# The first stage of a transformer layer reordered: inputs loaded in another order, one tile's modulation moved from TensorE to VectorE, and two blocks normalized from a transposed copy

## The chip, the cores and the metric

The kernel runs on one core of a Trainium2 chip. The metric is the time of one execution in microseconds (us) of device time; for the kernel before it is the median of three runs. Engines are called as the profile does: PE is TensorE's matmul, PEld its weight load, DVE VectorE, ACT ScalarE, POOL GpSimd, SP the engine that issues the DMAs. A transpose is a matmul against the identity matrix and so runs on PE.

## The reference

One layer of a transformer trunk, one sequence of S = 2048 tokens, D = 1024 features, everything in float32. Cut to what is computed:

```python
mod_all = einsum('bd,lde->lbe', silu(c), ada_w) + ada_b        # six rows of 1024
sh_m, sc_m, gt_m, sh_f, sc_f, gt_f = split(mod_all)
h = rms_norm(x, g0) * (1 + sc_m) + sh_m                        # norm over the 1024 features
y = stick_breaking_attention(h)                                # 16 heads of 64, w_qkv, w_o
x = x + gt_m * rms_norm(y, g1)
h = rms_norm(x, g2) * (1 + sc_f) + sh_f
x = x + gt_f * rms_norm(swiglu(h), g3)                         # w_in, w_out
```

The change lies in the first three lines and in what follows them at once, the products of h with the query, key and value weights. The modulation is 1 + scale times the gain (`g_eff`, one number for each feature) and the shift (`mod`).

## The kernel before

**Layout and precision.** The 2048 tokens are four blocks b = 0 to 3 of 512; the 1024 features are eight tiles k (or m) = 0 to 7 of 128. The products want h with the features on the 128 partitions, so a tile of h is 128 features x 512 tokens. Every float32 product is made of three matmuls on halves: each operand is split into a high part (a cast, on ACT) and a low part (a subtraction, on DVE or POOL), and `mm3` (L174 to L176) adds high x high, high x low and low x high. Three such rows are called a triple below. The heads go by pairs p = 0 to 7; t = 1, 0, 2 are the projections to k, q and v, in that order.

**The start, block 0** (L776 to L930). `row_load(m)` fetches the columns of ada_w for feature tile m, shift and scale, 512 KB each (ar). For the first `COLUMNS` tiles (three) the sums over c are made on PE as 16 matmuls of 128x1 a tile (`column`, L708, acol); for the other tiles DVE multiplies the rows with silu(c), spread over all partitions (c_rows), and adds up (`row_sum`, L716). silu(c) is made by ACT's Silu function; the spreading is done by two matmuls with ones (cs, L806). `row_done` makes mod and g_eff of the tile. Block 0's x comes by tokens (x0_0 to x0_3): `x_square` makes the squares' sum on ACT and the reciprocal root on POOL, `x_scale` multiplies on DVE, `turn_x(m)` transposes a tile by four transposes on PE, `full(m)` applies g_eff and mod on ACT, `high(m)` casts and `low(m)` subtracts. `products(p, m)` then issues the triples of tile m for the head pairs p = 0 and 1.

**Block 1 and block 3, by features** (`BY_FEATURES`). The host lays out a second copy of x with the features first (xt); its tiles (xc) need no transposes. Only the row of reciprocal roots has to come from x by tokens: the square sums of four token tiles (L165), each spread to 128 columns (`x_spread`, L340), four transposes to one row on all partitions (xr, `x_share`, L352) and a copy by ACT (L354). Then `scale_cols` multiplies xc by g_eff and the row (L372 on DVE, L376 on POOL) and `modulate` adds the shift with the cast (L389, L394, L395) and subtracts (L390, L397).

**Block 2, by tokens.** Its four token tiles are squared on ACT (xj, L165), scaled in place on DVE (L338), and transposed by 32 transposes on PE (xT2, L361), four ahead of each use; ACT applies g_eff and mod (L383), DVE casts and subtracts (L384, L385).

**What sets the order.** The instructions of PE, ACT, DVE and POOL run in the order in which the program writes them, each engine in order by itself; an engine that waits holds all that stands behind it on that engine. The start is straight-line code. From there on a loop goes through steps (p, b), each with t = 1, 0, 2 and k = 0 to 7 (`project`); block 1's step with p = 0 follows the start, then blocks 2 and 3; `first_norm(b, k)` makes the tiles of the next block beside the products of the present one. From block 1's t = 2 on, attention work of earlier blocks is put between the triples: scores z, the scan w (DVE), the product a (POOL), transposes t and their halves aT (ACT and DVE), the outputs o. SP issues the DMAs in program order, and each buffer's load waits until its earlier reader is done.

Of the kernel before, what the change touches and what calls it, by code (L numbers as in the profile page):

```python
# [16 lines left out]
P = 128  # L17
D = 1024
# [21 lines left out]
COLUMNS = 3  # L40
# [32 lines left out]
BY_FEATURES = (1, 3)  # L73
# [29 lines left out]
def hybrid_trunk_kernel(  # L103
# [25 lines left out]
    nc.vector.memset(lead, 0.0)  # L129
# [159 lines left out]
    x_tiles, x_norm, x_rstd, x_cols, x_row = {}, {}, {}, {}, {}  # L289

    x_places = {}

    def x_place(b):
        if b not in x_places:
            x_places[b] = [
                att.tile([P, 2, D], F32, name=f"x{b}_{i}", tag="qt", bufs=BUFS["qt"]) for i in range(2)
            ]
        return x_places[b]

    def x_load(b, *which):  # L300
        for i in which or range(4):
            r0 = b * BT + i * P
            if b == 2:
                tok = x_place(b)[i // 2][:, i % 2]
            else:
                tok = att.tile([P, D], F32, name=f"x{b}_{i}", tag="v", bufs=BUFS["v"])
            nc.sync.dma_start(tok, x[r0 : r0 + P])
            x_tiles[b, i] = tok

    def cols_load(b, *which):  # L310
        for m in which or range(KC // 2):
            cols = att.tile([P, 2, BT], F32, name=f"xc{b}_{m}", tag="kt", bufs=BUFS["kt"])
            nc.sync.dma_start(cols, xt[b // 2, :, 2 * m : 2 * m + 2])
            x_cols[b, 2 * m], x_cols[b, 2 * m + 1] = cols[:, 0], cols[:, 1]

    def x_square(b, i):
        if b > 0:
            tok = x_tiles[b, i]
            if b in BY_FEATURES:
                junk = tok  # L320
            else:
                junk = att.tile([P, D], F32, name=f"xj{b}_{i}", tag="wraw", bufs=BUFS["wraw"])
            x_rstd[b, i] = rms_scale(att, tok, f"n0_{b}_{i}", junk=junk)
            return
        xn = att.tile([P, D], F32, name=f"xn{b}_{i}", tag="kt", bufs=BUFS["kt"])
        x_norm[b, i] = xn
        x_rstd[b, i] = rms_scale(att, x_tiles[b, i], f"n0_{b}_{i}", junk=xn)

    def x_scale(b, i):
        nc.vector.tensor_scalar(  # L330
            x_norm[b, i], x_tiles.pop((b, i)), x_rstd.pop((b, i)), None, op0=ALU.mult
        )

    def x_spread(b, i):

        if b not in BY_FEATURES:
            tok = x_norm[b, i] = x_tiles.pop((b, i))
            nc.vector.tensor_scalar(tok, tok, x_rstd.pop((b, i)), None, op0=ALU.mult)  # L338
            return
        nc.vector.tensor_scalar(  # L340
            x_tiles[b, i][:, :P], ones, x_rstd.pop((b, i)), None, op0=ALU.mult
        )

    def x_share(b):

        if b not in BY_FEATURES:
            return
        pool, tag = (tps, "t") if b < 2 else (accps, "acc")
        pt = pool.tile([P, BT], F32, name=f"xr{b}", tag=tag)
        for i in range(4):  # L350
            tok = x_tiles.pop((b, i))
            nc.tensor.transpose(pt[:, i * P : (i + 1) * P], tok[:, :P], ident)  # L352
        x_row[b] = tok[:, BT:]
        nc.scalar.copy(x_row[b], pt)  # L354

    def x_turn(b, k):

        pool, tag = (tps, "t") if b == 0 else (accps, "acc")
        pt = pool.tile([P, BT], F32, name=f"xT{b}_{k}", tag=tag)
        for i in range(4):  # L360
            nc.tensor.transpose(  # L361
                pt[:, i * P : (i + 1) * P], x_norm[b, i][:, k * P : (k + 1) * P], ident
            )
        return pt

    def scale_cols(b, k):

        if b not in BY_FEATURES:
            return
# [8 lines left out]
    def modulate(hl, b, k):  # L378

        gain, add = g_eff[:, 0, k : k + 1], mod[:, 0, k : k + 1]  # L380
        if b not in BY_FEATURES:
            u = att.tile([P, BT], F32, name=f"hf{b}_{k}", tag="tmp", bufs=BUFS["tmp"])
# [1375 lines left out]
```

## Time and profile before

| | us |
|---|---|
| median of three runs (lowest, highest) | 2849.67 (2843.75, 2851.95) |
| the profiled execution, its own time | 2845.32 |
| its span, first to last instruction | 2843.2 |
| PE busy in the span | 2800.4 |
| DVE, ACT, POOL busy | 2021.7, 1634.1, 1282.5 |
| first triple of products starts | 24.45 |
| first triple of block 1 starts | 61.44 |
| first triple of block 2 starts | 88.56 |
| last triple of block 2's t = 0 starts | 109.47 |

The page's lines name an engine, the program's line, the operation, what it writes and reads (the numbers of tiles left out), how long it was busy, and what ended the idle time just before it. All times are counted from the start of the span. What lies outside the span (2845.32 against 2843.2) is 2.1 us in this execution. The table's last four rows are PE's marks for the stages that the change touches: everything that the change moves stands ahead of 109.47; from there on, the order of PE, DVE and ACT is the same in both programs.

### The profile page before, as it was taken

The page shows a single profiled execution, that of the slowest core. Times are in us where ns is not written, and L with a number is a line of the kernel's source. Part 1 is how long each engine was busy: PE and PEld are TensorE (multiplying, and loading weights), DVE is VectorE, ACT ScalarE, POOL GpSimd, SP SyncE. Part 2 cuts the span into 40 slices and gives each one's busy share as a digit, 9 for nine tenths or more (in the row PEclk, how much of TensorE's full clock was granted, in tenths as well). Part 3 has the DMA queues.
Part 4 walks back from the last instruction along what each step waited for, and adds up shares of the span by engine and source line. Part 5 has one row for each costly group of instructions (what it writes and reads, how often), then busy time and mean ns, then how long its engine had stood idle before and what let it go on. Part 6 is the DMA issues. An engine that isn't in the chain of part 4 may idle for free.

```text
span 2843.2 us, 41829 instructions
## 1 busy us (share of the span) xinstructions
PE 2800.4 (98%) x13853; PEld 2338.5 (82%) x13853; DVE 2021.7 (71%) x2822; ACT 1634.1 (57%) x3274; POOL 1282.5 (45%) x2032
## 2 busy tenths in 40 slices
PE   9899999999999999999999999999999999999998
PEld 7788888888888888887888788888788888888887
DVE  6788888888888888888866766555775655134377
ACT  5787778787777877778645533333433333322243
POOL 0565666676576655666410122222222222544454
PEclk9999999999999999999999999999999999999999
DMA  9774556666665635546389644334453335545575
GB/s 368 285 230 157 186 170 212 211 188 216 196 217 177 218 116 175 193 136 228 97 293 317 196 139 153 120 103 160 127 176 110 112 105 166 191 138 153 181 227 187
DMA packets 239787, 521.05 MB, mean 183 GB/s; under 512 B 22481, under 2 KB 108497, under 8 KB 222674
## 3 DMA queue, kind: packets, MB, share of 16 engines
q1 hardware_dynamic: 239570, 518.38, 56.4%
q8 instruction: 109, 1.79, 0.3%
q14 instruction: 108, 0.88, 0.1%
HBM read 351.04 MB, written 118.49 MB: 165 GB/s over the span
## 4 chain that ended last, share of the span: by engine, by line
PE 84%; DVE 5%; DMA 5%; ACT 2%; issue 2%; POOL 1%; SPq 0%; DVEq 0%; POOLq 0%; ACTq 0%
PE s L174 9%; PE s L175 9%; PE s L176 9%; PE z L593 8%; PE o L672 8%; PE t L644 8%; PE pj L174 5%; PE pj L176 5%; PE pj L175 5%; PE o L176 4%; PE o L174 4%; PE o L175 4%; DMA h_s<-ht 1%; PE y L176 1%; PE y L174 1%
## 5 line engine op out<-in xcount | busy, mean ns | idle before, releaser
L634 POOL TENSOR_TENSOR a<-a,w 128x512 f32<-128x512 f32 (+3 forms) x640 | 621.6, 971 | 217.2 <-DVE w L627 130.3
L627 DVE TENSOR_TENSOR_SCAN w<-z,c,begin 128x512 f32<-128x512 f32 x384 | 489.3, 1278 | 83.9 <-ACT z L612 60.6
L174 PE MATMUL s<-r,l 128*128 128x512 f32 x1232 | 482.3, 391 | 5.1 <-DVE p L1490 3.9
L176 PE MATMUL s<-r,l 128*128 128x512 f32 x1232 | 480.2, 390 | 0.0
L175 PE MATMUL s<-r,l 128*128 128x512 f32 x1232 | 479.9, 390 | 0.0
L610 ACT ACTIVATE a<-z 128x512 f32<-128x512 f32 (+3 forms) x640 | 347.1, 542 | 170.4 <-PE z L593 137.6
L672 PE MATMUL o<-aT,v 128*128 128x512 f32 (+3 forms) x1280 | 385.0, 382 | 0.1
L660 DVE TENSOR_TENSOR aT<-t,aT 128x512 fp32r<-128x512 f32 (+3 forms) x640 | 358.6, 594 | 23.9 <-ACT aT L654 23.4
L593 PE MATMUL z<-kt,qt 128*128 128x512 f32 (+3 forms) x1280 | 363.7, 365 | 0.0
L654 ACT CAST aT<-t 128x512 fp32r<-128x512 f32 (+3 forms) x640 | 313.9, 533 | 73.5 <-PE t L644 63.4
L612 ACT ACTIVATE z<-z 128x512 f32<-128x512 f32 (+3 forms) x640 | 344.8, 539 | 0.0
L1498 POOL TENSOR_TENSOR one<-p,p 128x512 f32<-128x512 f32 x44 | 70.9, 1612 | 579.1 <-issue 322.2
L174 PE MATMUL pj<-ht,w 128*128 128x512 f32 x768 | 308.4, 402 | 4.3 <-issue 1.4
L644 PE MATMUL t<-begin,a 128*128 128x128 f32 x2176 | 295.7, 274 | 13.8 <-DVE aT L660 12.5
L644 PEld LDWEIGHTS t<-begin,a 128*128 128x128 f32 x2176 | 255.7, 141 | 64.1 <-DVE aT L660 14.0
L175 PE MATMUL pj<-ht,w 128*128 128x512 f32 x768 | 301.5, 393 | 2.0 <-DVE ht L390 1.5
L176 PE MATMUL pj<-ht,w 128*128 128x512 f32 x768 | 301.9, 393 | 0.0
L174 PEld LDWEIGHTS s<-r,l 128*128 128x128 f32 x1232 | 231.7, 188 | 56.0 <-ACT l L1351 2.9
L176 PEld LDWEIGHTS s<-r,l 128*128 128x128 f32 x1232 | 231.5, 188 | 48.3
L175 PEld LDWEIGHTS s<-r,l 128*128 128x128 f32 x1232 | 231.7, 188 | 48.0 <-issue 0.5
L622 DVE TENSOR_TENSOR_SCAN w<-z,begin 128x128 f32<-128x128 f32 (+3 forms) x256 | 208.6, 817 | 76.7 <-ACT z L612 67.5
L593 PEld LDWEIGHTS z<-kt,qt 128*128 128x128 f32 x1280 | 231.0, 189 | 37.6 <-DVE w L622 0.2
(178 smaller groups left out, 4879.3 us busy)
## 6 DMA issues: line engine op xcount, KB each, us to landing
ht<-h_s SPq DMA_DIRECT2D x108, 1024.0 KB, 8.2
wi<-in_win SPq DMA_DIRECT2D x86, 512.0 KB, 4.0
qt<-qn SPq DMA_DIRECT2D x124, 256.0 KB, 4.8
ol_qt<-act_s SPq DMA_DIRECT2D x56, 512.0 KB, 3.7
act_s<-S SPq DMA_DIRECT2D x66, 256.0 KB, 4.1
br<-in_wout SPq DMA_DIRECT2D x66, 256.0 KB, 3.5
h_s<-ht SPq DMA_DIRECT2D x16, 1024.0 KB, 9.8
o_s<-os SPq DMA_DIRECT2D x128, 128.0 KB, 2.6
```

The source lines that it names most:

```text
L174: nc.tensor.matmul(acc, lhs[0], rhs[0], start=first, stop=False, **kw)
L175: nc.tensor.matmul(acc, lhs[0], rhs[1], start=False, stop=False, **kw)
L176: nc.tensor.matmul(acc, lhs[1], rhs[0], start=False, stop=last, **kw)
L593: nc.tensor.matmul(z[:, :n], q[:, e, part, r * P : (r + 1) * P], k[:, e, :n], start=part == 0, stop=part == 1,)
L610: nc.scalar.activation(a[:, :n], z[:, :n], AF.Sigmoid, scale=QK_SCALE)
L612: nc.scalar.activation(z[:, :n], z[:, :n], AF.Sigmoid, scale=-QK_SCALE)
L627: nc.vector.tensor_tensor_scan(rest[:, rev], left[:, rev], begin[:, :BT][:, rev], initial=carries[r], op0=ALU.mult, op1=ALU.bypass,)
L634: nc.gpsimd.tensor_tensor(a[:, :n], a[:, :n], rest[:, 1 : n + 1], op=ALU.mult)
L644: nc.tensor.transpose(pt[:, rb * P : (rb + 1) * P], weighed[i, rb][:, j * P : (j + 1) * P], ident)
L654: nc.scalar.copy(hl[:, 0, t0:], pt[:, t0:])
L660: nc.vector.tensor_tensor(hl[:, 1, t0:], pt[:, t0:], f32(hl[:, 0, t0:]), op=ALU.subtract)
L672: nc.tensor.matmul(acc[:, t0:], lhs, hl[:, part, t0:], start=sc == qb and j == 0 and part == 0, stop=sc == 0 and j == 3 and part == 1,)
```

## The change

**Loads.** b_cols and gc (biases and gains) and x0 come right after c; the columns of ada_w follow. Block 1's x by tokens and its xc come in another order; block 2 has no tokens any more but four xc tiles, and block 3 has no tokens either. 2 MB less is loaded net.

**silu.** It is c times sigmoid(c): ACT makes the sigmoid of c (128x8) and, later, of the spread c (two of 128x512 into c_rows), DVE multiplies. The Silu function is used nowhere, and one of three loads of an ACT table goes away.

**Columns.** `COLUMNS` is 2 in place of 3: tile 2's sums go from 16 matmuls on PE to two `row_sum` on DVE. Tile 1's two columns stand behind the first triple and the second triple of products, one each.

**Block 1's row sooner.** The squares of block 1's tokens stand between the tiles of block 0, and the row (`x_share(1)`) and the first two tiles stand ahead of `products(0, 6)` in place of behind it.

**Blocks 2 and 3 by features alone.** The square sums of a block come from xc: ACT squares four pairs of tiles (128x1024 each, xs, `cols_square`), DVE adds them up in four additions (three of 128x1024, one of 128x512, `cols_add`), PE adds over the partitions by four matmuls of 128x1 (xq, `cols_sum`), and four spreads, four transposes (xr) and a copy make the row as for block 1. Three tables place them in the loop. Block 3's third and fourth pair of squares are written to one and the same buffer as its second. Block 2's 32 transposes, and the scaling and the squares by tokens of both blocks, go away. Block 2's odd tiles are scaled by POOL, and modulated and cast by ACT.

```diff
-COLUMNS = 3
+COLUMNS = 2
-BY_FEATURES = (1, 3)
+XSQUARE_AT = {2: {(1, 2): 0, (1, 3): 1, (1, 6): 2, (1, 7): 3}, 3: {(1, 4): 0, (1, 5): 1, (0, 0): 2, (0, 2): 3}}
+XADD_AT = {2: {(1, 5): 1, (1, 7): 2, (0, 0): 3, (0, 1): 4}, 3: {(1, 7): 1, (0, 1): 2, (0, 3): 3, (0, 4): 4}}
+XSUM_AT = {2: [(0, 2), (0, 3), (0, 5)], 3: [(0, 5), (0, 6), (0, 7)]}
...
+    def cols_square(b, m):
+        if m == 0 or (m == 2 and b == 2):
+            both = att.tile([P, 2, 2, BT], F32, name=f"xs{b}_{m}", tag="qt", bufs=BUFS["qt"])
+            x_squares.setdefault(b, []).extend([both[:, 0], both[:, 1]])
+        elif m > 1 and b == 3:
+            x_squares[b].append(x_squares[b][1])
+        nc.scalar.activation(x_squares[b][m], x_pairs.pop((b, m)), AF.Square)
+
+    def cols_add(b, m):
+        total = x_squares[b][0]
+        if m < KC // 2:
+            nc.vector.tensor_tensor(total, total, x_squares[b][m], op=ALU.add)
+        else:
+            nc.vector.tensor_tensor(total[:, 0], total[:, 0], total[:, 1], op=ALU.add)
+
+    def cols_sum(b):
+        total = x_squares.pop(b)[0]
+        ps = accps.tile([P, BT], F32, name=f"xq{b}", tag="acc")
+        for i in range(4):
+            nc.tensor.matmul(
+                ps[:, i : i + 1], total[:, 0, i * P : (i + 1) * P], ones[:, 0:1], start=True, stop=True
+            )
...
-                square_at = {2: 0, 3: 1}.get(nb)
-                if t == square_at and k < 4:
-                    x_square(nb, k)
-                if t == square_at and 2 <= k < 6:
-                    x_spread(nb, k - 2)
-                if nb and (t, k) == (0, 1):
-                    x_share(nb)
...
+                if nb:
+                    if (t, k) in XSQUARE_AT[nb]:
+                        cols_square(nb, XSQUARE_AT[nb][t, k])
+                    if (t, k) in XADD_AT[nb]:
+                        cols_add(nb, XADD_AT[nb][t, k])
+                    if (t, k) in XSUM_AT[nb]:
+                        (cols_sum, x_spread, x_share)[XSUM_AT[nb].index((t, k))](nb)
...
     nc.sync.dma_start(c_act, c)
-    row_load(0)
-    nc.sync.dma_start(c_line[0:1], c_row)
-    x_load(0)
     nc.sync.dma_start(b_cols, ada_b_cols)
     nc.sync.dma_start(gc, g_cols)
-    row_load(1)
+    x_load(0, 0)
+    x_load(0, 1)
+    nc.sync.dma_start(c_line[0:1], c_row)
+    x_load(0, 2)
+    x_load(0, 3)
+    row_load(0)
     load_weights(0, 1)
     load_weights(0, 0)
+    row_load(1)
     load_weights(0, 2, "kt")
+    load_weights(1, 1, "v")
     row_load(2)
...
+    products(0, 0, 1)
+    column(1, 0)
     weights_high(0, 0)
-    high(0)
+    weights_low(0, 0)
+    products(0, 0, 0)
+    column(1, 1)
+    weights_high(0, 2)
+    weights_low(0, 2)
+    weights_high(1, 1)
+    row_done(1)
...
+    products(0, 5)
+    for i in range(3):
+        x_spread(1, i)
...
+    products(1, 5)
+    x_share(1)
+    cols_load(2, 3, tag="v")
+    first_norm(1, 0)
+    first_norm(1, 1)
     products(0, 6)
-    x_share(1)
     products(1, 6)
     products(0, 7)
-    first_norm(1, 0)
-    first_norm(1, 1)
     products(1, 7)
```

PE at the very start. Before, the first rows are tile 0's columns, the spread of c, tile 1's columns, and the turns of block 0's tiles:

```order
L708 MATMUL acol_163<-c_act_76,ar0_167 128x1 x16
L806 MATMUL cs0_227<-c_line_164,ones_68 128x512
L806 MATMUL cs1_228<-c_line_164,ones_68 128x512
L708 MATMUL acol_163<-c_act_76,ar1_181 128x1 x16
L361 MATMUL xT0_0_298<-begin_62,xn0_0_232 128x128
```

After, the spread of c stands first, then tile 0's columns, then the turns:

```order
L805 MATMUL cs0_209<-c_line_164,ones_68 128x512
L805 MATMUL cs1_210<-c_line_164,ones_68 128x512
L703 MATMUL acol_163<-c_act_76,ar0_178 128x1 x16
L366 MATMUL xT0_0_267<-begin_62,xn0_0_229 128x128
L366 MATMUL xT0_0_267<-begin_62,xn0_1_236 128x128
```

The columns of tile 1 are gone from this place; behind the turns of tiles 0 and 1 it goes on with the first two triples (ht0_0_0 is the normed h of block 0, pj a projection's sum), and the columns stand between and behind them:

```order
L178 MATMUL pj0_0_1_264<-ht0_0_0_284,w0_1_279 128x512
L179 MATMUL pj0_0_1_264<-ht0_0_0_284,w0_1_279 128x512
L180 MATMUL pj0_0_1_264<-ht0_0_0_284,w0_1_279 128x512
L703 MATMUL acol_163<-c_act_76,ar1_185 128x1 x8
L178 MATMUL pj0_0_0_265<-ht0_0_0_284,w0_0_300 128x512
L179 MATMUL pj0_0_0_265<-ht0_0_0_284,w0_0_300 128x512
L180 MATMUL pj0_0_0_265<-ht0_0_0_284,w0_0_300 128x512
L703 MATMUL acol_163<-c_act_76,ar1_185 128x1 x8
```

So the first triple has moved ahead of tile 1's 16 column matmuls.

DVE in block 1's products, behind the last two tiles of block 1's norm (ht0_1_3); v and kn are halves of projections of block 0 and block 1. Before, it works on block 2's tokens:

```order
L546 TENSOR_TENSOR v0_0_718<-vt0_0_713,v0_0_718 128x8x64
L546 TENSOR_TENSOR v1_0_732<-vt1_0_727,v1_0_732 128x8x64
L496 TENSOR_TENSOR kn0_1_745<-pj0_1_1_689,kn0_1_745 128x512
L167 TENSOR_SCALAR n0_2_0_ms_765<-n0_2_0_ssq_763 128x1
L167 TENSOR_SCALAR n0_2_1_ms_775<-n0_2_1_ssq_773 128x1
L167 TENSOR_SCALAR n0_2_2_ms_785<-n0_2_2_ssq_783 128x1
L338 TENSOR_SCALAR x2_0_531<-x2_0_531,n0_2_0_rstd_767 128x1024
```

After, the additions of block 2's squares stand there, with kn between them:

```order
L541 TENSOR_TENSOR v0_0_714<-vt0_0_709,v0_0_714 128x8x64
L541 TENSOR_TENSOR v1_0_737<-vt1_0_732,v1_0_737 128x8x64
L326 TENSOR_TENSOR xs2_0_701<-xs2_0_701 128x1024
L326 TENSOR_TENSOR xs2_0_701<-xs2_0_701,xs2_2_745 128x1024
L491 TENSOR_TENSOR kn0_1_755<-pj0_1_1_683,kn0_1_755 128x512
L326 TENSOR_TENSOR xs2_0_701<-xs2_0_701,xs2_2_745 128x1024
L328 TENSOR_TENSOR xs2_0_701<-xs2_0_701 128x512
L338 TENSOR_SCALAR xm2_777<-xq2_772 128x4
```

The scaling of block 2's tokens has gone, and four additions stand in its place, the last of them ahead of the row's own steps (xm2).

PE in block 1's t = 0, which reads those sums two triples in (nothing like it stood there before):

```order
L178 MATMUL pj0_1_0_763<-ht0_1_0_601,w0_0_300 128x512
L179 MATMUL pj0_1_0_763<-ht0_1_0_601,w0_0_300 128x512
L180 MATMUL pj0_1_0_763<-ht0_1_0_601,w0_0_300 128x512
L334 MATMUL xq2_772<-ones_68,xs2_0_701 128x1 x4
L178 MATMUL pj0_1_0_763<-ht0_1_1_646,w0_0_300 128x512
```

The other six triples of t = 0 now stand behind a matmul that reads DVE's last addition.

DVE and PE in block 2's t = 0. Before, DVE has the scans w and the halves aT of the attention, one behind the other (the scans are listed as SCALAR_TENSOR_TENSOR):

```order
L660 TENSOR_TENSOR aT0_0_1078<-t0_0_1062,aT0_0_1078 128x512
L496 TENSOR_TENSOR kn0_2_1087<-pj0_2_1_924,kn0_2_1087 128x512
L660 TENSOR_TENSOR aT0_1_1099<-t0_1_1067,aT0_1_1099 128x384
L622 SCALAR_TENSOR_TENSOR w1_3_1102<-z1_3_1081,begin_62 128x512
L622 SCALAR_TENSOR_TENSOR w2_0_1129<-z2_0_1109,begin_62 128x128
L660 TENSOR_TENSOR aT0_2_1138<-t0_2_1124,aT0_2_1138 128x256
L660 TENSOR_TENSOR aT0_3_1153<-t0_3_1127,aT0_3_1153 128x128
```

After, the additions of block 3's squares (xs3) stand among them:

```order
L655 TENSOR_TENSOR aT0_0_994<-t0_0_978,aT0_0_994 128x512
L326 TENSOR_TENSOR xs3_0_956<-xs3_0_956 128x1024
L491 TENSOR_TENSOR kn0_2_1004<-pj0_2_1_902,kn0_2_1004 128x512
L655 TENSOR_TENSOR aT0_1_1017<-t0_1_983,aT0_1_1017 128x384
L617 SCALAR_TENSOR_TENSOR w1_3_1020<-z1_3_997,begin_62 128x512
L326 TENSOR_TENSOR xs3_0_956<-xs3_0_956 128x1024
L617 SCALAR_TENSOR_TENSOR w2_0_1043<-z2_0_1027,begin_62 128x128
L655 TENSOR_TENSOR aT0_2_1052<-t0_2_1038,aT0_2_1052 128x256
L326 TENSOR_TENSOR xs3_0_956<-xs3_0_956 128x1024
L328 TENSOR_TENSOR xs3_0_956<-xs3_0_956 128x512
```

Four additions have come in between the halves that PE's outputs o wait for.

and PE reads their sum before it goes on:

```order
L667 MATMUL o0_0_0_1055<-aT0_1_1017,v0_0_714 128x384 x2
L588 MATMUL z2_2_1083<-kt0_1_758,qt0_1_814 128x384 x2
L334 MATMUL xq3_1086<-ones_68,xs3_0_956 128x1 x4
L178 MATMUL pj0_2_0_1012<-ht0_2_2_921,w0_0_300 128x512
L179 MATMUL pj0_2_0_1012<-ht0_2_2_921,w0_0_300 128x512
```

The last three triples of t = 0 stand behind it.

More of the change, by code (lines that the diff above doesn't have):

```diff
@@ L326, in x_square @@
[L326 to L342, printed above, removed]
+        junk = x_tiles[b, i]
@@ L344, in x_share, with x_spread @@
+    def x_spread(b, *which):
+        if b not in x_spreads:
+            x_spreads[b] = att.tile([P, 4, P], F32, name=f"xw{b}", tag="tmp", bufs=BUFS["tmp"])
+        for i in which or range(4):
+            rstd = x_rstd[b][:, i : i + 1] if b > 1 else x_rstd.pop((b, i))
+            nc.vector.tensor_scalar(x_spreads[b][:, i], ones, rstd, None, op0=ALU.mult)
     def x_share(b):
-        if b not in BY_FEATURES:
-            return
+        spread = x_spreads.pop(b)
         pool, tag = (tps, "t") if b < 2 else (accps, "acc")
```

220 lines of the change are left out of this document (98 added, 122 removed).

## The prediction

> **What bounds the kernel now.** I read the page's head first, then busy time by stage, then the clock in the 3.41 us steps in which it changes, then PE's, DVE's and ACT's timelines in the first 125 us.
>
> ```profile
> span 2843.2 us, 41829 instructions
> PE 2800.4 (98%) x13853; PEld 2338.5 (82%) x13853; DVE 2021.7 (71%) x2822; ACT 1634.1 (57%) x3274; POOL 1282.5 (45%) x2032
> PE 84%; DVE 5%; DMA 5%; ACT 2%; issue 2%; POOL 1%; SPq 0%; DVEq 0%; POOLq 0%; ACTq 0%
> ```
>
> PE is busy for 98% of the span and holds 84% of the chain that ended last, so the time moves by what PE does or waits for. By stage (each row: stretch, length, busy time and count of PE, PEld, DVE, ACT, POOL, then granted clock, DMA share, GB/s):
>
> ```profile
> 0.00:24.45 24.45, 19.23 (x100) 16.80 (x101) 8.41 (x21) 14.87 (x22) 4.71 (x11) 0.93 0.92 356
> 24.45:61.44 36.99, 36.99 (x183) 30.85 (x182) 28.71 (x60) 20.78 (x33) 2.20 (x4) 1.00 1.02 415
> 61.44:88.56 27.12, 23.83 (x109) 18.62 (x109) 17.95 (x34) 15.01 (x30) 4.22 (x8) 0.94 0.95 323
> 88.56:100.13 11.57, 10.77 (x58) 7.97 (x57) 11.12 (x24) 11.15 (x23) 5.77 (x13) 1.00 1.00 369
> 100.13:109.47 9.34, 9.34 (x54) 8.03 (x53) 6.69 (x11) 5.47 (x14) 4.95 (x15) 1.00 1.00 337
> ```
>
> The rows are the start, block 0's products, block 1's, block 2's t = 1 and t = 0. PE is never idle in the second and the last, loses 3.3 us in the third and 0.8 in the fourth, where ACT is busy for 11.15 of 11.57. Behind 109.47 the orders are alike, so I take that part as unchanged, within 2 us.
>
> **The start.** Before:
>
> ```profile
> 5.20 6.96 PE L708 MATMUL acol<-c_act,ar 128*128 128x1 f32 x32 [5.20 <-DMA ar<-in_ada_cols_first]
> 12.02 3.76 PE L806 MATMUL cs<-c_line,ones 128*128 128x512 f32 x4
> 24.45 0.48 PE L174 MATMUL pj<-ht,w 128*128 128x512 f32 x1
> 25.91 1.84 PE L708 MATMUL acol<-c_act,ar 128*128 128x1 f32 x16
> 35.05 0.39 PE L174 MATMUL pj<-ht,w 128*128 128x512 f32 x1
> 12.43 1.06 ACT L165 ACTIVATE xn<-x 128x1024 f32<-128x1024 f32 x1 [0.17 <-DMA x<-in_x]
> 28.24 0.78 ACT L757 ACTIVATE hf<-xT,mod,g_eff 128x512 f32<-128x512 f32 x1 [0.74 <-DVE g_eff L723]
> 29.06 0.62 ACT L768 CAST ht<-hf 128x512 fp32r<-128x512 f32 x1
> 30.35 1.22 DVE L742 TENSOR_TENSOR w<-wr,w 128x1024 fp32r<-128x1024 f32 x1
> 31.49 1.22 DVE L716 SCALAR_TENSOR_TENSOR ar<-ar,c_rows 128x1024 f32<-128x1024 f32 x1
> 32.63 0.68 DVE L772 TENSOR_TENSOR ht<-hf,ht 128x512 fp32r<-128x512 f32 x1
> ```
>
> Before, the last of x0's four loads came sixth among the 512 KB loads, at about 12.3 (row 12.43, released by it). Now x0 is first and tile 0's second half of columns is the sixth, so it lands at about 12.3 too. A tile's columns take 6.96 at the half clock of row 5.20 and 3.7 at full clock (2 x 1.84, row 25.91). Starting one load (512 KB at 415 GB/s, 1.26 us) sooner, at 11.0, they end between 14.7 and 18.0; I take 16. The spread of c, 3.76, fits ahead of them. Tile 0's gain, modulation (0.78), cast (0.62) and subtraction (0.68) add 2.4: first triple at 18.4 where it was at 24.45. The Silu function's table load and the loads of biases lie beside this wait and I cost them at nothing; if the columns came sooner, ACT's squares of x0 would be next.
>
> This 6 us is not kept. Tile 1's columns now stand behind the first two triples, 1.84 to 3.5 us each (half of 3.7, half of 6.96), so its gain is there at 18.4 + 2 x 0.69 + 2 x 2.6 + 0.8 = 25.8 (24 to 28). Behind that gain DVE has, in order, three low parts of weights (1.15 each, from the pitch of rows 30.35 and 31.49), one subtraction (0.6), two sums of tile 2 (1.15 each), their addition (0.4) and the first sum of tile 3 (1.15): 8 us that before lay partly under the 24.45. Tile 2's triples, which follow PE's own work here, start at 25.8 + 8.2 + 1 = 35.0, and before at 35.05. From there PE was never idle to 61.44, and has one turn more to do than it had (four transposes, 0.4). Block 0's products end at about 61.85: **front +0.4 us**, with ends of -1.9 and +2.2 from the two clocks.
>
> **Block 1.** Before:
>
> ```profile
> 55.47 0.59 ACT L354 COPY x<-xr 128x512 f32<-128x512 f32 x1 [2.01 <-PE xr L352]
> 56.09 2.08 DVE L372 SCALAR_TENSOR_TENSOR xc<-xc,g_eff,x 128x512 f32<-128x512 f32 x3 [1.43 <-ACT x L354]
> 66.57 0.49 PE L175 MATMUL pj<-ht,w 128*128 128x512 f32 x1 [1.53 <-DVE ht L390]
> 69.09 1.28 DVE L546 TENSOR_TENSOR v<-vt,v 128x512 fp32r<-128x512 f32 x2
> 71.22 0.39 PE L174 MATMUL pj<-ht,w 128*128 128x512 f32 x1
> 72.68 1.06 ACT L165 ACTIVATE xj<-x 128x1024 f32<-128x1024 f32 x1 [2.00 <-DMA k_park<-kn]
> 78.00 0.33 PE L361 MATMUL xT<-begin,x 128*128 128x128 f32 x1 [0.71 <-DVE x L338]
> 84.69 0.60 PE L361 MATMUL xT<-begin,x 128*128 128x128 f32 x4
> 77.31:80.73 3.42, 1.90 (x8) 1.35 (x9) 2.71 (x5) 1.03 (x2) 1.22 (x2) 1.00 1.01 417
> 80.73:84.14 3.41, 3.41 (x13) 2.81 (x12) 1.96 (x4) 1.11 (x3) 0.00 (x0) 0.50 1.00 393
> ```
>
> Block 1's row moves ahead of a group of three triples (3 x 0.685), so it is some 1.95 us sooner. That is more than the 1.53 that PE waited at 66.57, so that wait goes. But DVE is saturated here: from 56.09 to the end of the v halves (70.37) it has 14.28 us of work in a row for block 1's norm. Now it starts 1.95 sooner, 7.3 us ahead of the first triple of block 1, and the v halves end 7.0 behind it; then come the four additions (three of 128x1024 at 1.15, one of 128x512 at 0.6) and one kn half (0.6), 4.7 us, and some 0.3 of waiting: 12.0 behind the first triple. The matmuls xq2 need the last of them, and PE gets there after ten triples of 0.685 and two turns of v of 0.35, at 7.55. PE waits 4.4 us, and does the sums in 0.5: 12.5, where before the same triple (71.22) came 9.78 in. ACT's four squares (1.06 each, row 72.68) hide beside this: ACT was busy for 15 of 27 us. Before, no such wait stood here; its price is bounded by nothing (the additions done in time) and by the 4.4.
>
> What goes away follows: from 71.22 to 88.56 PE had 17.34 us; the four groups of block 2's transposes there (0.36 each by row 84.69 and its successor), the three waits for DVE's scaling (0.71 the longest) and the half clock of 80.73 to 84.14 (1.7 us lost) leave about 12.0 with the new row's four transposes. Block 2 starts 24.5 behind block 1, before 27.12.
>
> A dip of the clock can come back: the stretch ahead of the dip had PE busy for 1.90 of 3.42. A wait of 4.4 us in one piece leaves some stretch with less than that. I take 1.7 us at 3 in 4: **+1.3**. [...]
>
> **Block 2.** Before, rows of the parts that come back in block 2's path:
>
> ```profile
> 107.17 0.96 DVE L622 TENSOR_TENSOR_SCAN w<-z,begin 128x384 f32<-128x384 f32 x1 [1.66 <-ACT z L612]
> 113.63 0.73 ACT L389 ACTIVATE ht<-xc,mod 128x512 fp32r<-128x512 f32 x1 [1.49 <-DVE xc L372]
> 116.92 0.81 ACT L394 ACTIVATE xc<-xc,mod,g_eff 128x512 f32<-128x512 f32 x1
> 117.77 0.62 ACT L395 CAST ht<-xc 128x512 fp32r<-128x512 f32 x1
> 121.25 1.79 DVE L372 SCALAR_TENSOR_TENSOR xc<-xc,g_eff,x 128x512 f32<-128x512 f32 x1
> 122.97 0.74 DVE L390 SCALAR_TENSOR_TENSOR ht<-xc,mod,ht 128x512 fp32r<-128x512 f32 x1
> ```
>
> In t = 1, ACT had 11.15 us. Five tiles by tokens (0.78 each) and four squares with their accumulators (1.24 each) go; two even tiles (0.73), three odd ones (0.81 + 0.62) and two squares (1.06) come: 11.15 - 8.9 + 7.9 = 10.1, and at the 96% that ACT kept, 10.5 us, before 11.57. PE loses 16 transposes and the waits for them, so ACT stays the bound.
>
> In t = 0 PE ran 9.34 us without a stop. The change puts four additions among the halves aT, and block 3's squares and additions take turns on one buffer: the third square waits for the first addition, the second addition for the third square, the fourth square for that, the third addition for it. Alone these are 4 additions (4.1) and 2 squares (2.1), with ACT's sigmoids (0.6 each) and DVE's scans (0.8) in between. Followed in order from the stage's start: first addition ends at 1.8, third square 2.9, second addition 6.0 behind a half and a scan, fourth square 7.5, third and fourth addition 10.2. PE waits on the way for the second half aT of the attention (2.3, behind the addition) and at xq3 for the last addition (3.5): 9.34 - 0 + 5.8 + 0.2 = 15.3. The bounds: 9.8 (all waits hidden in DVE's slack, row 107.17 has 1.66 of it) and 15.3. I take 15.3, since the chain of turns on one buffer has no slack that I can find.
>
> **Sum.** Before, block 2's t = 0 ended 48.03 behind block 1's start. After: 24.5 + 10.5 + 15.3 = 50.3: +2.3. With the front +0.4 and the dip +1.3: **+4.0 us**. The profiled execution took 2845.32 (span 2843.2 and 2.1 outside), 4.35 below the median 2849.67; on the median's footing 2853.7. About 0.3%, 8.5 us, is what a measurement of this kernel can tell from no change, so this is no change.
>
> **Rivals.** First, the sums are in time: if neither xq2 nor xq3 waits (DVE's idle 1.66 at 107.17 speaks for it, its 14.28 us without a gap before 70.37 against), the stages take 8.05 + 12.0, 10.5 and 10.2, together 40.8 where they took 48.03: -7.3, with the front -6.9, so 2842.8; with the front's best end 2840.5, which counts as faster. I give it 2 in 10.
>
> Second, slower: PE stays at half clock through the start. Now PE pauses until the columns land at 11, and works on short columns and transposes behind that. Before, it was at half clock in one such place:
>
> ```profile
> 19.29:22.70 3.41, 3.39 (x17) 3.00 (x17) 2.13 (x4) 2.41 (x4) 0.00 (x0) 0.50 1.02 406
> 22.70:26.10 3.40, 3.40 (x26) 3.15 (x26) 3.10 (x5) 3.40 (x5) 0.00 (x0) 1.00 1.03 408
> ```
>
> If the columns, turns and first triples all run at half clock, tile 1's gain comes at 30.5 (18 + 2.4 + 0.6 for the turns + 2 x 1.3 + 2 x 3.5), 4.7 later than taken: +9.1 in all, 2858.8, slower. It decides only if the clock is still half at about 24; row 22.70, full clock behind a stretch that was mostly transposes, speaks against. [...] I give it 1 in 10.
>
> Third, DVE against POOL: one multiplication on DVE took 1.79 where its like took 0.74 (row 122.97), while POOL multiplied a tile too. Block 2's four odd tiles on POOL now lie beside DVE's chain: up to 4 x 1.05 = 4.2 more, +8.2, 2857.9. [...] I give it 1.5 in 10. The remaining 5.5 is the forecast, 2848 to 2859 by itself (the front's ends, the dip).
>
> That the change does not do what it says is excluded by the order: the transposes are gone and the additions are there.
>
> **The numbers.** The range reaches from the first rival's best (2841) to the second rival with half of the third (2863). Faster: half of the first rival, 0.10, and 0.07 for the front at its best end with waits that are half as long as I took. Slower: the second rival, half of the third, and a tenth or so of the forecast where its waits add to a dip twice, 0.24. Same: 0.59.
>
> **What would show it.** First triple at 18 to 19; PE's third tile at about 35; a wait of PE for DVE's additions of about 4 us at xq2, 3 to 4 at xq3 and 2 at aT in block 2; block 2's t = 1 with ACT above 95%. Wrong I am if PE reaches the sums and does not wait (then the first rival), if the clock's row at 22 to 26 is 0.50 (the second), or if the part behind the last triple of t = 0 does not come out alike.

## The result and the profile after

The changed kernel takes 2862.93 us (median of four runs, 2861.17 to 2863.77) against 2849.85 for the kernel before beside it: 1.0046 times, 95% interval 1.003 to 1.0061. It is slower, by 13 us, where 2853.7 was forecast and no change held the largest chance (0.59). The time lies at the very edge of the range (2841 to 2863).

The page of the changed kernel, its head, and its busy time by the same stages as before (start up to the first triple, block 0, block 1, block 2's t = 1 and t = 0, the rest; columns as in the prediction):

```profile
span 2860.8 us, 41725 instructions
PE 2803.4 (98%) x13809; PEld 2339.3 (82%) x13809; DVE 2032.0 (71%) x2827; ACT 1633.3 (57%) x3269; POOL 1284.1 (45%) x2030
...
17.80:64.65 46.85, 46.78 (x204) 39.13 (x205) 36.40 (x73) 24.66 (x37) 2.30 (x4) 0.85 1.00 395
64.65:93.03 28.38, 23.75 (x105) 19.24 (x104) 18.68 (x30) 14.30 (x26) 4.39 (x6) 0.88 1.00 348
93.03:106.18 13.15, 9.68 (x43) 7.60 (x41) 10.79 (x11) 10.80 (x20) 7.46 (x12) 0.87 0.97 361
106.18:126.48 20.30, 13.43 (x62) 10.84 (x60) 12.74 (x20) 7.86 (x18) 6.32 (x14) 0.83 0.20 60
```

The granted clock, third from the right, is below 0.9 in all four stages; before it was 1.00 in three of the four and 0.94 in block 1's. Read against before:

| stage | before | after | difference | forecast |
|---|---|---|---|---|
| start and block 0 | 61.44 | 64.65 | +3.2 | +0.4 |
| block 1 | 27.12 | 28.38 | +1.3 | -1.3 |
| block 2, t = 1 | 11.57 | 13.15 | +1.6 | -1.1 |
| block 2, t = 0 | 9.34 | 20.30 | +11.0 | +6.0 |
| rest of the span | 2733.7 | 2734.3 | +0.6 | 0 |

The sum is 17.6, the difference of the spans. It is more than the medians' 13.1 because the profiled execution of before (2845.32) was one of its quicker ones. One correction to what stands ahead: the mark 109.47 is the first triple of block 2's t = 2, not the last of t = 0; the stage that ends there is t = 0 all the same, and 126.48 is the same triple after.

Where PE stood or crawled in the changed kernel, from its timeline (start, length, engine, line; in brackets the idle time before and what ended it):

```profile
19.55 3.41 PE L703 MATMUL acol<-c_act,ar 128*128 128x1 f32 x16
24.24 3.41 PE L703 MATMUL acol<-c_act,ar 128*128 128x1 f32 x16
76.98 1.86 PE L334 MATMUL xq<-ones,xs 128*128 128x1 f32 x8 [4.41 <-DVE xs L328]
97.17 0.50 PE L179 MATMUL pj<-ht,w 128*128 128x512 f32 x1 [1.15 <-DVE ht L394]
100.45 0.79 PE L179 MATMUL pj<-ht,w 128*128 128x512 f32 x1 [2.31 <-DVE ht L387]
111.56 0.33 PE L639 MATMUL t<-begin,a 128*128 128x128 f32 x1 [2.73 <-DVE aT L655]
118.81 1.86 PE L334 MATMUL xq<-ones,xs 128*128 128x1 f32 x8 [4.15 <-DVE xs L328]
```

The program's 128x1 matmuls stand twice each in these rows: x16 is one column of eight matmuls, x32 a tile's two columns, and x8 the four sums. PE waits for DVE's last addition at both sums, 4.41 and 4.15, as forecast (4.4 and 3.5), for the halves aT (2.73, forecast 2.3), and twice for block 2's norm (1.15 and 2.31, not forecast). And what follows a wait runs slowly: the four short sums took 1.86. The clock, first over five of its steps of 3.41 us together and over one of these, then two pairs of steps (the columns are those of the stages):

```profile
15.21:32.27 17.06, 16.39 (x61) 14.26 (x62) 9.77 (x15) 6.77 (x8) 0.00 (x0) 0.51 1.03 409
22.03:25.45 3.42, 3.42 (x15) 3.13 (x14) 0.00 (x0) 0.00 (x0) 0.00 (x0) 0.50 1.02 407
...
73.23:76.64 3.41, 0.00 (x0) 0.00 (x0) 3.37 (x4) 0.43 (x1) 0.00 (x0) 0.97 1.04 434
76.64:80.06 3.42, 3.08 (x11) 2.87 (x12) 0.44 (x2) 0.00 (x0) 0.94 (x1) 0.50 1.01 424
...
114.19:117.60 3.41, 0.47 (x3) 0.15 (x1) 1.84 (x4) 3.17 (x9) 1.73 (x5) 0.97 0.00 0
117.60:121.01 3.41, 2.20 (x9) 2.20 (x10) 2.08 (x5) 0.02 (x1) 0.83 (x3) 0.50 0.01 2
```

Behind each step in which PE did little (0.00 and 0.47 us) stands one at half clock: that was expected. The first two rows are the riddle: PE is busy for 16.39 of 17.06 us and is granted half. Of the step 22.03 to 25.45 it is busy for all; what it does there is, for the greater part (2.0 of 3.42), the columns of tile 1, 128x1 matmuls. The kernel before has such a step too, with PE busy throughout on 128x1 columns; it is the one ahead of its step at half clock, 19.29 to 22.70:

```profile
15.87:19.29 3.42, 3.42 (x32) 3.42 (x33) 0.75 (x1) 1.54 (x2) 0.35 (x1) 1.00 1.03 416
```

### The profile page after: what moved, and what is told of

The parts are those of the page before. It is cut to its first block, busy times and chain, and to the rows that moved or that the text cites. A ratio compares the mean times of both kernels' runs of the same rounds, so it can differ in the third digit from the quotient of the medians.

```text
span 2860.8 us, 41725 instructions
## 1 busy us (share of the span) xinstructions
PE 2803.4 (98%) x13809; PEld 2339.3 (82%) x13809; DVE 2032.0 (71%) x2827; ACT 1633.3 (57%) x3269; POOL 1284.1 (45%) x2030
## 4 chain that ended last, share of the span: by engine, by line
PE 87%; DVE 4%; ACT 2%; issue 1%; DMA 1%; POOL 1%; SPq 0%; DVEq 0%; POOLq 0%; ACTq 0%
PE s L178 9%; PE s L180 9%; PE s L179 9%; PE z L588 8%; PE o L667 8%; PE t L639 8%; PE pj L178 5%; PE pj L180 5%; PE pj L179 5%; PE o L180 5%; PE o L178 5%; PE o L179 5%; PE y L180 2%; PE y L178 2%; PE y L179 2%
## 5 line engine op out<-in xcount | busy, mean ns | idle before, releaser
L639 PEld LDWEIGHTS t<-begin,a 128*128 128x128 f32 x2176 | 256.1, 141 | 66.5 <-DVE aT L655 17.2
```

The costliest lines, as they stand in the source:

```text
L639: nc.tensor.transpose(pt[:, rb * P : (rb + 1) * P], weighed[i, rb][:, j * P : (j + 1) * P], ident)
```

## The experiments

All edits are to the kernel named; ratios are to the kernel before, from runs beside it. The marks "block 1 at" and so on are PE's first triples of a stage.

**1 and 2. Which half of the change costs.** The changed start with the loop of before (the diff is against the changed kernel),

```diff
-    cols_load(2, 0, 1, tag="v")
+    x_place(2)
+    x_load(2)
...
-                    if (t, k) in XSQUARE_AT[nb]:
-                        cols_square(nb, XSQUARE_AT[nb][t, k])
...
+                square_at = {2: 0, 3: 1}.get(nb)
+                if t == square_at and k < 4:
+                    x_square(nb, k)
```

> The changed start (loads, columns, silu by the sigmoid, block 1's row sooner) with the loop of before: blocks 2 and 3 come by tokens again. Theory (the loss is mostly the sums of blocks 2 and 3, the start loses a few us to the half clock): block 0's products end 3.2 us later than before, block 1's row comes some 2 us sooner relative to that, so the wait of 1.5 at block 1's norm goes: 1 to 3 us slower than before, so the comparison shows no difference that can be told. Rival (the start's later end also delays blocks 2 and 3 through loads and buffers, and most of the 13 us hangs on it): 8 us or more slower than before.

and the start of before with the changed loop (the second line is against the kernel before):

```diff
-COLUMNS = 2
+COLUMNS = 3
...
-    x_load(2)
+    cols_load(2, 0, 1, tag="v")
```

> The start of before with blocks 2 and 3 by features alone. Theory: block 0's products end at 61.4 as before; block 1's row is not sooner, so DVE's chain starts 2 us later and the wait at the first sums (4.4 us in the changed kernel) grows to 6 to 7; the stages of block 2 lose 1.6 and 11 us as in the changed kernel; 14 to 17 us slower than before, no better than the whole change. Rival (the start carries most of the loss): under 8 us slower than before.

Measured: the start alone 2848.47, ratio 0.9988 (0.9977 to 0.9999); the loop alone 2862.88, 1.0043 (1.0028 to 1.0059), 12 us, a little under the 14 to 17 expected. So the whole loss is that of blocks 2 and 3, and the start costs nothing; if anything it gains 3 us, less than the 0.3% that the prediction took for the least that can be told. In the start's trace block 1 begins at 65.20, 3.8 later than before, and most of this is given back: block 1 takes 23.77 in place of 27.12,

```profile
65.20:88.97 23.77, 21.83 (x110) 17.43 (x108) 15.97 (x30) 14.48 (x29) 4.24 (x8) 1.00 1.00 335
```

without the 1.53 us wait at its norm, which the sooner row takes away, and without the half clock, which does not go with the row (experiment 7's trace has the wait and no half clock, experiment 6's the sooner row and a half clock, 0.93). By block 2's t = 2 this execution is still 2.2 us behind (111.65 for 109.47), and the rest of it is 4.0 shorter; so it is the times of ten runs, not this one trace, that say the start costs nothing. The loop alone repeats the waits at the sums, to a few hundredths in spite of the later row; the 6 to 7 expected for the first missed, since PE now waits at block 1's norm ahead of it. Its start, the code of before, ended at 64.35 in the traced execution, not at 61.44, with columns at half clock. The two waits:

```profile
69.50 0.50 PE L179 MATMUL pj<-ht,w 128*128 128x512 f32 x1 [1.56 <-DVE ht L387]
78.70 1.87 PE L334 MATMUL xq<-ones,xs 128*128 128x1 f32 x8 [4.39 <-DVE xs L328]
```

**3. The turns on one buffer.** Block 3's third and fourth squares get buffers of their own:

```diff
         elif m > 1 and b == 3:
-            x_squares[b].append(x_squares[b][1])
+            x_squares[b].append(att.tile([P, 2, BT], F32, name=f"xs{b}_{m}", tag="wraw", bufs=BUFS["wraw"]))
```

> The changed kernel with one thing undone: block 3's third and fourth squares go to buffers of their own, so ACT's squares no longer wait for DVE's additions. Theory (the turns on one buffer make the wait at the second sums): the fourth square comes 3 to 5 us sooner, the wait of 4.15 us at xq3 falls to under 2 us, block 2's t = 0 takes 17 us in place of 20.3, 2 to 4 us faster than the changed kernel. Rival (DVE's own queue, with scans and halves that wait for ACT, makes the wait): the third and fourth square move but the last addition ends within 1 us of where it did, no gain.

Measured: 2858.57, 1.0024 (1.0015 to 1.0034), 4.4 us under the changed kernel, a little more than the 2 to 4 expected. Block 2's t = 0 takes 14.43 in place of 20.30. PE's wait there, its columns at the start, and the fourth square on ACT, first in the changed kernel, then here:

```profile
12.42 6.96 PE L703 MATMUL acol<-c_act,ar 128*128 128x1 f32 x32 [1.42 <-DVE n_ms L171]
...
119.35 1.05 PE L334 MATMUL xq<-ones,xs 128*128 128x1 f32 x8 [2.14 <-DVE xs L328]
...
114.43 1.06 ACT L321 ACTIVATE xs<-xc 128x1024 f32<-128x1024 f32 x1 [2.52 <-issue]
...
113.04 1.08 ACT L321 ACTIVATE xs<-xc 128x1024 f32<-128x1024 f32 x1
```

The wait fell from 4.15 to 2.14, that at aT from 2.73 to 1.42, and the sums run at full clock (1.05 in place of 1.86). In the changed kernel ACT stood 2.52 us ahead of that square, which begins as DVE's second addition ends (114.34); here it does not wait. The turns on one buffer were half of PE's wait; DVE's queue is the other half: DVE works here without a gap from 109.94 until the last addition ends at 119.29. Not all of the 20.30 to 14.43 is the buffers', though. The loop alone, with the turns, had waits of 1.51 at aT and 4.16 at the sums, the sums at full clock, and 18.16 for the stage. Counted from the start of the stage, the sums come after 9.32 here and after 11.44 to 12.73 in the four traces with turns. The first row shows something else. The start is the same code as the changed kernel's, where these 32 matmuls took 3.85 at full clock; here they took 6.96, and block 1 began at 68.70 in place of 64.65. So the start differs by 4 us between two executions. What makes the difference is not shown; PE also stood 1.42 us ahead of these columns here, and 0.36 there.

**4 and 10. Why PE is at half clock while busy.** The column matmuls made 128 wide, and 16 wide, by spreading silu(c) first (`WIDE`); the count of matmuls and the weights are the same, and the sum is there 128 or 16 times over:

```diff
-                out_col, w[:, k], c_act[:, k : k + 1], start=k == 0, stop=k == KC - 1,
+                out_col, w[:, k], c_wide[k], start=k == 0, stop=k == KC - 1,
...
+    for k in range(KC):
+        nc.vector.tensor_scalar(c_wide[k], ones[:, :WIDE], c_act[:, k : k + 1], None, op0=ALU.mult)
```

> The changed kernel with the column matmuls made 128 columns wide in place of one (the same sum 128 times over, from silu(c) spread by eight short multiplications on DVE); the same count of matmuls and weights. Theory (the clock's gate counts a 128x1 matmul as next to nothing, so that tile 1's columns, though PE shows as busy, hold the clock at half from 15 to 32): granted clock 1.00 from about 19 on, columns behind the first triples 2 us each in place of 3.4, tile 1's gain at 23 to 25 in place of 27.9, block 0's products end 3 to 5 us sooner, total 3 to 5 us faster than the changed kernel. Rival (what holds the clock is that PE paused for the loads until 11, or the transposes): the clock's rows stay at 0.50 up to 28, no gain.

> The changed kernel with column matmuls 16 wide, to set beside 1 and 128. Theory (the gate weighs the columns that stream through the array, not the instruction's time): 16 columns are still an eighth of the instruction's time, so the half clock from 15 to 32 stays as with 1, 2861 to 2864. Rival (any change of the operand, or the eight short DVE instructions ahead of it, set the clock free): full clock as with 128, 2857 to 2860.

Measured: 128 wide 2859.14, 1.0027 (1.0016 to 1.0037), 3.8 us under the changed kernel, with intervals that meet; 16 wide 2860.54, 1.0039 (1.0023 to 1.0056), whose interval holds the changed kernel's 1.0046. The traces are plainer than the times. The step of 22 to 25 and the first columns behind a triple, 128 wide:

```profile
22.03:25.45 3.42, 3.42 (x25) 2.86 (x24) 1.53 (x4) 1.27 (x3) 0.00 (x0) 1.00 1.02 408
...
19.27 1.95 PE L706 MATMUL acol<-c_wide,ar 128*128 128x128 f32 x16
```

and 16 wide:

```profile
22.03:25.45 3.42, 3.42 (x16) 3.32 (x17) 1.92 (x2) 0.57 (x1) 0.00 (x0) 0.50 1.03 412
...
21.56 3.43 PE L706 MATMUL acol<-c_wide,ar 128*128 128x16 f32 x16
```

PE is busy for the whole step in both (3.42 of 3.42), and is granted all of the clock in the one (1.00) and half of it in the other (0.50). What sets the clock here is therefore not the time that the profile shows as busy but how many columns wide the matmuls are. The fourteen traces of this case agree: the seven with columns 1 or 16 wide all have half clock behind their first columns, for 3.4 us or more of the first 37 (in experiments 3 and 5 the clock's rows show 1.00 there, and it is told by the 3.41 us that 16 matmuls took); in the seven with 64 or 128 wide everything from the first transposes to 37 runs at full clock. It is not that only large matmuls count: in the kernel before, the step 19.29 to 22.70, mostly 128x128 transposes, was followed by full clock (1.00 from 22.70 to 26.10). At full clock a 128-wide column matmul costs hardly more than a 1-wide one did (1.95 for 16, where the 128x1 ones of before took 1.84). What the start gains by wide columns is less than the clock gives: block 1 begins at 63.19 in place of 64.65 (66.75 with 16), 1.5 sooner where 3 to 5 was expected, since PE now waits for DVE in block 0, 3.6 us in all, where the changed kernel has no such wait. The longest:

```profile
46.01 0.50 PE L181 MATMUL pj<-ht,w 128*128 128x512 f32 x1 [2.18 <-DVE ht L770]
```

It also makes the start steadier: with the changed start, block 1 begins between 64.65 and 68.70 in the five traces with narrow columns, and between 63.02 and 63.40 in the four with wide ones.

**5. The sums later.** With own buffers, and these places (the norms of the other blocks keep theirs):

```diff
-XSUM_AT = {2: [(0, 2), (0, 3), (0, 5)], 3: [(0, 5), (0, 6), (0, 7)]}
+XSUM_AT = {2: [(2, 0), (2, 1), (2, 3)], 3: [(0, 7), (2, 0), (2, 2)]}
-NORM_AT = [(2, 2), (2, 4), (2, 6)]
+NORM_AT = {2: [(2, 3), (2, 5), (2, 7)]}
```

> The changed kernel with block 3's third and fourth squares in buffers of their own, and with the sums later: block 2's in t = 2 of block 1 (k = 0, 1, 3, its first norm one slot later), block 3's at k = 7 of t = 0 and k = 0 and 2 of t = 2. Theory (what the features cost is PE's waiting for sums, with the half clock behind each wait, and no more): the waits at xq2 (4.4) and xq3 (2.1 with own buffers) fall to under 1 us and no half clock follows; 5 to 8 us faster than with own buffers alone, so 2851 to 2854, within 0.2% of before. Rival (the squares, additions and odd tiles load DVE, ACT and POOL so that the time comes back as waits for block 2's norm): the waits for ht in block 2's t = 1 grow by 4 us or more, no gain beyond 2 us.

Measured: 2851.58, 1.0002 (0.9992 to 1.0013): 7.0 under own buffers alone, and as fast as before. Of the waits at the sums 0.31 is left, at block 2's; block 1 takes 23.37 and block 2's t = 0 11.56. Most of what is left is in block 2's t = 1:

```profile
91.43:105.72 14.29, 11.02 (x43) 8.17 (x41) 12.50 (x15) 11.41 (x21) 8.29 (x12) 0.76 1.01 365
...
99.09 0.80 PE L179 MATMUL pj<-ht,w 128*128 128x512 f32 x1 [2.31 <-DVE ht L387]
```

The wait for block 2's norm did not grow, it stayed at 2.31, with a stretch at half clock behind it.

**6 and 7. Wide columns with the start of the change, and in the kernel before.** The edit of experiment 4 in the first experiment's kernel (128 wide) and in the kernel before (64 wide, three tiles):

```diff
+WIDE = 64
...
+        nc.vector.tensor_scalar(c_wide[k], ones[:, :WIDE], c_act[:, k : k + 1], None, op0=ALU.mult)
```

> The changed start with the loop of before, and columns 128 wide. Theory (the 128x1 columns hold the clock at half): no row at half clock between 19 and 32, block 0's products end 1.5 to 4 us sooner than with the changed start alone, 2845 to 2848 where that had 2848.5: faster than before by 0.1 to 0.25%. Rival (the start is bound by DVE's low parts and row sums, so PE only waits elsewhere): full clock, but the end of block 0's products moves by less than 1 us, no gain.

> The kernel before with its three tiles' columns 64 wide and nothing else. Theory: the half clock at 19 to 23 goes, tile 2's columns (2.2) shorten, block 0's products end 1 to 3 us sooner; 0 to 3 us faster. Rival (the window that dipped held mostly transposes, and these do not count): the half clock stays, no gain.

Measured: 2844.71, 0.9975 (0.9965 to 0.9986), and 2843.36, 0.9969 (0.9959 to 0.9978). The edit alone makes the kernel before 0.31% faster, more than the 0 to 3 us that were expected, and, with the second try of experiment 9, the fastest here. In the profile it shows less than in the times: the first triple comes at 22.56 in place of 24.45 and the half clock of 19 to 23 is gone, but block 1 begins at 61.51, and before at 61.44. What it changes is the spread: ten runs lie within 3.8 us (2841.54 to 2845.36), where 31 runs of the kernel before lay within 14.3 (2844.59 to 2858.87). Where the longer executions of before lose their time, and so where most of the 0.31% comes from, isn't shown, since none of them was traced. The start is one place: in the two traces of the same start it ended at 61.44 and 64.35. The rest of the span is another: behind block 2's t = 0 it took 2729.82 in experiment 5's trace and 2737.31 in experiment 8's, with the same order there; the latter execution was the longest of its kernel (2852.01).

**8. All three together.** Wide columns, own buffers, later sums:

> The changed kernel with all three: wide columns, own buffers for block 3's squares, later sums. Theory: the gains add up, 3 to 5 us for the clock at the start to those of own buffers and later sums: 2847 to 2850, as fast as before or a little faster. Rival (block 0's products are bound by DVE, so the clock's gain is not kept): no better than own buffers and later sums without it.

Measured: 2846.73, 0.9984 (0.9975 to 0.9994). The gains add up: 4.9 under the same without wide columns, and in the traces block 1 begins at 63.40 in place of 68.06. Features for blocks 2 and 3, freed of their waits, are still not ahead of tokens (experiments 6 and 7; experiment 6's interval meets this one).

**9. DVE against POOL, and block 1's row.** Two more edits, one in the kernel of experiment 8: block 2's odd tiles as block 1's, on DVE and one ACT instruction,

```diff
-        if k % 2 == 0 or b == 1:
+        if k % 2 == 0 or b in (1, 2):
```

> The changed kernel with wide columns, own buffers and later sums, and block 2's odd tiles scaled on DVE with the shift and cast in one ACT instruction (as block 1's) in place of POOL and two ACT instructions. Theory (DVE and POOL hold each other up when both read two tiles, as the third rival had it): DVE's instructions of 1.6 to 1.8 us in block 2's t = 1 go back to 0.7, the wait of 2.31 for ht goes to under 0.7, and block 2's t = 1 takes 11 to 12 us in place of 13.3: 1 to 2.5 us faster than without it. Rival (the wait is a late row, or ACT): the wait for ht stays at 2 us or turns into another of that size, no gain.

Measured: 2844.53, 0.998 (0.9971 to 0.9988), 2.2 under experiment 8, with intervals that meet. But the wait for the norm did not go as the theory wanted. DVE's slowest norm instruction there, and PE's waits:

```profile
91.50 1.57 DVE L389 SCALAR_TENSOR_TENSOR ht<-xc,mod,ht 128x512 fp32r<-128x512 f32 x1
...
89.85 0.54 PE L181 MATMUL pj<-ht,w 128*128 128x512 f32 x1 [1.49 <-DVE ht L389]
93.13 0.79 PE L181 MATMUL pj<-ht,w 128*128 128x512 f32 x1 [1.89 <-DVE ht L389]
```

One instruction of 1.57 is left, beside POOL's product a of the attention (91.08, 1.45 long), and there are two waits of 1.49 and 1.89 in place of one of 2.31. Block 2's t = 1 takes 14.65 in place of 13.28; what was gained lies ahead of it (block 1 takes 21.45 in place of 23.34, with 0.30 in place of the 1.51 that PE waited for v). So POOL's tiles alone are not the limit of t = 1 with features. DVE's longer queue is the likely one; the edit takes POOL's tiles away and adds them to that queue, so it does not separate the two.

The other, in the kernel before with wide columns: of the change, only block 1's row sooner, by the changed order of squares, row and first tiles:

```diff
+    x_share1(1)
+    first_norm(1, 0)
+    first_norm(1, 1)
     products(0, 6)
-    x_share(1)
     products(1, 6)
     products(0, 7)
-    first_norm(1, 0)
-    first_norm(1, 1)
     products(1, 7)
```

> The kernel before with wide columns and, of the change, only block 1's row sooner (its tokens' buffers and squares as in the changed start, the row and its first two tiles ahead of the group of triples they stood behind). Theory (what the changed start gains is the 1.56 us wait at block 1's norm): that wait goes, 1 to 2 us faster than wide columns alone, 2841 to 2843, 0.3 to 0.4% faster than before. Rival (DVE's row sums are late, so squares and row wait for them): block 0's products end later by 1 us or more, no gain.

Measured: 2847.96, 0.9994 (0.9985 to 1.0004), 4.6 slower than wide columns alone. The squares were put ahead of tokens that had not landed:

```profile
46.23 1.06 ACT L167 ACTIVATE x<-x 128x1024 f32<-128x1024 f32 x1 [9.18 <-DMA x<-in_x]
...
48.22 0.79 PE L177 MATMUL pj<-ht,w 128*128 128x512 f32 x1 [4.51 <-DVE ht L796]
```

ACT waited 9.18 us for them, DVE for ACT, and PE 4.51 for DVE. A second try loads the tokens ahead of block 1's feature tiles and squares them a place later:

> As the last one (before, wide columns, block 1's row sooner), but block 1's tokens are loaded ahead of its feature tiles and squared one place later, so that DVE does not wait for the loads. Theory: no wait of PE in block 0's products, the 1.56 us at block 1's norm goes, 2841 to 2843. Rival (the loads still come too late for an earlier row): a wait of 1 us or more in block 0's products or at the row, 2843.5 or slower, no gain over wide columns alone.

Measured: 2843.70, 0.9979 (0.997 to 0.9989): no gain over wide columns alone that can be told. In its trace there is no wait in block 0, the one at block 1's norm is gone, and block 2's t = 2 begins at 107.62 where before it was 109.47; wide columns alone had 110.52 in the one execution that was traced.

## Why the prediction was right or wrong

- **The waits at the sums: right.** xq2 4.41 for 4.4, xq3 4.15 for 3.5, aT 2.73 for 2.3. The chain of turns that the prediction followed is in the trace step by step: first addition, third square, second addition, fourth square and last addition end 3.2, 4.4, 8.2, 9.3 and 12.6 into the stage, where it said 1.8, 2.9, 6.0, 7.5 and 10.2. Experiment 5 takes the waits for the sums away (0.31 is left) and the time comes back to that of before (1.0002), from 1.0046.
- **The reason at xq3: half right.** The prediction put it down to the turns on one buffer; they made 2 of its 4 us (experiment 3), and DVE's scans and halves the rest.
- **The price of a wait: the step that failed most.** The forecast took a wait at its own length and one dip at 1.3 us. Measured, the waits for both sums had two steps at half clock behind them (76.6 to 83.5 and 117.6 to 124.4), and block 2's norm had one; the wait for aT had none. At xq2: the sums 1.72 where 0.5 was priced (+1.2), three triples 3.99 together in place of 2.06 (+1.9) and the row's transposes 0.65 in place of 0.36 (+0.3): 3.4 us where 1.3 was priced. At xq3: the sums 1.73, at full clock 0.91 (+0.8), two triples of 1.35 (+1.3) and seven transposes of 1.18 in place of 0.68 (+0.5): 2.6 us where nothing was priced; and the sums at full clock were priced at 0.2, not 0.91 (+0.7). With the waits in t = 0 1.1 longer than said, that makes 19.7 of the 20.30 measured there, where 15.3 was forecast.
- **Block 2's t = 1: wrong.** It was costed as bound by ACT, 10.5 at 96%. ACT was busy for 10.80 of 13.15; PE waited 3.46 for DVE's norm and lost 1.5 to the clock (100.45 to 103.80: 3.35 us for work of 1.85 at full clock). DVE took 1.58, 1.76 and 1.82 us for instructions of 0.7, beside POOL's multiplications, which the third rival had said; taking POOL's tiles away (experiment 9) did not remove the waits, so this rival is not the whole cause either.
- **The start: the first triple right, the rest not.** 17.80 for 18.4; but tile 2's triples at 37.79 for 35.0, since the clock was at half up to 32. The second rival's condition held (0.50 at 22 to 26), with a smaller price than it said: block 1 at 64.65, not 66.5. (Its +9.1 counts the front's 0.4 twice; 4.0 and 4.7 make 8.7, 2858.4.) Of the three things that it named, the pause for the loads, the short columns and the transposes, it is the columns that held the clock (experiments 4 and 10). And the loss of 3.2 us is not what made the kernel slower: with the loop of before the same start is no slower (experiment 1), for block 1 gives 3.4 back, 1.5 by the row that comes sooner and the rest by a half clock that this execution did not have.
- **The part behind the last triple of t = 0: right,** 0.6 us for 0.
- **The footing: a cause of error of some 4 us in the other direction.** The sum was made against a profiled execution 4.35 under the median. By the spans the change costs 17.6 us, by the medians 13.1; the forecast of +4.0 is short by 13.6 of the former. That 2862.93 lies inside the range, by 0.07, is luck: this error ran against the others, and the range's upper end was added up from the second and third rivals, not from the half clock behind the waits.

## What to carry to other kernels

A wait of PE, which bounds this kernel, cost its own length and up to two steps of 3.41 us at half clock behind it (0.50 and 0.53 behind the wait of 4.41); price both. In these traces busy time alone did not keep the clock up: 128x1 matmuls, even back to back (PE busy for all of 15.87 to 19.29), were followed by half clock (0.50), and widening them to 64 or 128 columns cost almost nothing (1.89 and 1.95 us for 16, in place of 1.84) and, with 64, gave 0.31% of a kernel of 2850 us by one edit. A sum that PE must take from DVE belongs where DVE's queue is through with it, which is found by adding up that queue from the last instruction it waited for.

## What the runs showed of the hardware

- Granted clock 0.51 over five steps in a row (15.2 to 32.3) while PE was busy 96% of that time, with matmuls of 128x1 among it, and 0.50 over six (13.4 to 33.8) with 128x16; 1.00 with 128x128 in the same places.
- The step of the kernel before in which PE was busy throughout with 128x1 matmuls (15.87 to 19.29) was followed by one at 0.50; the next, mostly 128x128 transposes, by 1.00.
- A column (x16 in the rows) took at full clock 1.84 us with 128x1, 1.89 with 128x64 and 1.95 with 128x128.
- The same start, in two executions, had its first two columns (x32) in 3.85 and in 6.96 us. In the second the clock's record shows 1.00 up to 80 us, though a column (x16) behind them took 3.41 where 1.84 is full clock: the matmuls' own durations tell the half clock, the record does not.
- A 128x512 instruction of DVE with two inputs took up to 1.82 us beside POOL's multiplication of tiles (95.30 in the changed kernel), and 0.69 without one (89.84).
